# Which queue brings the identity, which transfers lead, and a hold on the first weight casts, in a two-layer attention and pooling block

## The chip, the cores and the metric

One core of a Trainium2 chip runs the whole program in one launch. The metric is device time in microseconds (us) of that launch; the time given for a kernel is the median of its runs. A profile is one further execution, recorded by the hardware profiler.

## What is computed

The reference puts 16 meta tokens ahead of 512 tokens of width 1024 and runs two layers over the 528 rows. Cut to what matters:

```python
h = concatenate([meta, x])                        # 528 x 1024
for l in range(2):
    n    = rms_norm(h, norm_gain[l])              # row / sqrt(mean(row^2) + 1e-6) * gain
    proj = n @ w_in[l]                            # 1024 x 4808, cut into ten parts:
    q, k, v, gate_a, u_b, gate_b, q_idx, k_idx, w_idx, merge = split(proj)
    q, k, q_idx, k_idx = rope(...)                # q and k are normed per head first
    attn = top-128 attention of q over k, v       # keys chosen by the q_idx, k_idx, w_idx scores
    y_a  = (attn * silu(gate_a)) @ w_a[l]
    y_b  = (multiscale_pool(u_b) * silu(gate_b)) @ w_b[l]
    g_a, g_b = split(sigmoid(merge))
    h    = h + (g_a * y_a + g_b * y_b) @ w_out[l]
return h[16:]
```

All in 32-bit floats. [...]

## The kernel before

**Layout.** Activations stand with the features on the partitions and the 528 tokens along the free dimension: `RES[0]` is 128 x 8 x 528, feature block by feature block. Since x comes from memory token by token, it is turned at the start. Tokens are cut into five tiles (`TOK`): tile 0 is the 16 meta tokens, tiles 1 to 4 are 128 tokens of x each, and the work is done in two halves, tiles 0 to 2 and tiles 3 to 4. `xt` holds the four tiles of x as they come from memory, `start` the meta rows and a scratch row for squares, `consts` the tables, whose first 128 columns are the 128 x 128 identity that every turn by TensorE needs.

**First transfers (lines 399 to 434).** SyncE's queue (SP in the profile) issues, in this order: the identity (L405), x tile 1 (L406), x tile 2 (L407), half of the key/value weights `raw` of the chunk `kv` (L156 through `w_fetch(kv, 0)`, two transfers), the rest of the tables (L428), the head gains (L429), the other half of that chunk (two transfers, L156), the two halves of the first index-query chunk `first` (L156, two transfers), and last x tiles 3 and 4 (L434, two transfers). ScalarE's queue (ACTq) issues the meta rows (L408) and the small parameter rows (L409) before ScalarE's first own work, the load of a function table. Each transfer reports on one of eight hardware semaphores, handed out in order of issue over both queues; a transfer that takes a semaphore in use waits on its issuing queue until the earlier transfer on that semaphore has landed.

**Meanwhile** TensorE runs 19 products of zeros (`spin(W0)`, L424) that keep it busy until x is there.

**Start of the work (lines 1163 to 1216).** `x_half(0)` squares and sums the rows of tiles 0, 1 and 2 (ScalarE L1183 and L1179, VectorE for half of tile 2) and takes 1/rms on GpSimd (`inv_rms`, L494 and L495). `x_turned(0)` turns tile 1, then the meta rows, then tile 2 on TensorE, eight transposes each, by way of the identity. `norm_half(0, 0, ...)` spreads 1/rms over the partitions with TensorE and then for each of the eight feature blocks lets VectorE make the normed block `nf` and ScalarE its high part `hhi` (L521); the low parts `hlo` follow on VectorE. The loop at L1209 copies the first 32 tokens of each group of four blocks to `nm` on ScalarE (L1211).

**First weights.** `plain_trio` (L1232) multiplies tiles 0 to 2 by the key/value chunk in plain 32-bit form. `w_prep_enqueue(True)` (L1234) puts the preparation of the chunk `first` in a queue of small steps that `chunk()` empties at L1235: `highs()` (L232) casts both halves to their high parts on ScalarE (`act.copy`, L206), then VectorE subtracts to get the low parts. `w_prep_enqueue` takes an argument `after`: an instruction behind which the scheduler must put these casts (`tc.issue_after`, L233). For this chunk it is not given; for the third chunk it is, at L1253. After that `x_half(1)` and `x_turned(1)` (L1238) do tiles 3 and 4, and the index queries of tiles 1, 2 and so on begin, each `tok_group` of 24 products.

**What sets the order.** TensorE and VectorE run their instructions in the order in which the code writes them (`manual_schedule`, L101). ScalarE, GpSimd and SyncE are ordered by the scheduler of the tile layer, from data dependences, its own estimate of when operands are there, and the edges that `issue_after` adds.

Of the kernel before, what the change touches and what calls it, by code (L numbers as in the profile page):

```python
# [18 lines left out]
NM = 16  # L19
# [72 lines left out]
def tile_block(ctx: ExitStack, tc: tile.TileContext, x, meta, w_in, pool_w, w_a, w_b, w_out, rows, hgain, c_tab, out):  # L92
    nc = tc.nc
    act, gp = nc.scalar, nc.gpsimd
# [8 lines left out]
    def f(ap):  # L103
        return ap.bitcast(F32)
# [53 lines left out]
    def w_load():  # L158
        if W["load"] < len(chunks):
            c = w_place()  # L160
            for s in range(2):
                w_fetch(c, s)
# [10 lines left out]
    def w_tile():  # L173
        return wpool.tile([128, 1024], F32R, tag="w", name="w", bufs=8)

    def w_prep_enqueue(casts_first=False, after=None):
        c = W["prep"]
        if c >= len(chunks):
            return
        W["prep"] += 1  # L180
        kt = chunks[c][0][0].shape[1]
        cols = 2048 // kt
        if c in plain:
            return
        ready[c] = {}
        if c in mixed:
            prep_q.extend(mixed_prep(c))
            return
        parts = ready[c] = ([], [])

        def split(which):
            if c == kept_chunk:
                if which not in own:
                    own[which] = one.tile([128, KT, 256], F32R, tag=("Ahi", "Alo")[which], name="wo")
                i = len(parts[which])
                t = own[which][:, i:i + kt // 2, :]
            else:
                t = w_tile().rearrange("p (k e) -> p k e", e=cols)
            parts[which].extend(t[:, k] for k in range(kt // 2))
            return t  # L200

        his, own = {}, {}

        def high(s):
            his[s] = split(0)
            act.copy(his[s], raws[c][s])  # L206

        def low(s):
            dve.tensor_sub(split(1), raws[c][s], f(his[s]))
            if s == 1:  # L210
                del raws[c]
                w_load()

        def second():
            low(0)
            high(1)

        def minus(s):
            t = split(1)
            act.activation(t, raws[c][s], AF.Copy, scale=-1.0)  # L220
            gp.dma_start(t, raws[c][s], accum_op=OP.add)  # L221

        def plus(s):
            t = split(0)
            act.copy(t, raws[c][s])  # L225
            if s == 1:
                del raws[c]
                w_load()
                with tc.issue_after(added[0]):
                    first_sum(c + 1)  # L230

        def highs():  # L232
            with tc.issue_after(after) if after else nullcontext():  # L233
                high(0)
                high(1)

        if casts_first:
            prep_q.extend((highs, lambda: low(0), lambda: low(1)))
        elif c in by_dma:
            prep_q.extend((lambda: minus(0), lambda: minus(1), lambda: plus(0)))  # L240
            if c in metas:
                prep_q.append(lambda: meta_queries(metas[c], raws[c]))
            prep_q.append(lambda: plus(1))
        else:
            prep_q.extend((lambda: high(0), second, lambda: low(1)))
# [7 lines left out]
    def first_sum(c):  # L253
        if c in mixed:
            gp.dma_start(raws[c][0][:, 1], raws[c][0][:, 0], accum_op=OP.add)  # L255
# [74 lines left out]
    def chunk(ahead=True):  # L330
        flush_prep()
        c = W["use"]
        W["use"] += 1
        if ahead:
            w_prep_enqueue()
        return ready.pop(c)
# [62 lines left out]
    consts = one.tile([128, NCOL], F32, name="consts")  # L399
# [2 lines left out]
    junk, mt = start[:, 0, :], start[:16, 1, :]  # L402
    dma = nc.sync.dma_start
    xt = one.tile([128, 4, D], F32, tag="C", name="xt")
    dma(consts[:, :128], c_tab[:, :128])  # L405
    dma(xt[:, 0, :], x[0, 0:128, :])  # L406
    dma(xt[:, 1, :], x[0, 128:256, :])  # L407
    act.dma_start(mt, meta)  # L408
    act.dma_start(par, rows)  # L409
    warm = one.tile([128, 1], F32, name="warm")  # L410
# [89 lines left out]
    NF = [None]  # L500
    NM = []
# [43 lines left out]
    def meta_queries(g, raw):  # L545
        ps = bank("d")
        by_columns(ps, 256, [(lambda k: NM[k // 4][:, k % 4, :], lambda k: raw[k // 4][:, k % 4, :])])
        dst = qm[:, 4 * g:4 * g + 4, :]
        later(lambda: meta_sum(ps, 256, lambda total: q_post(0, total, True, dst, g)), 1)
# [658 lines left out]

    for b in range(2):  # L1209
        NM.append(tmp.tile([128, 4, 32], F32, tag="pm", name="nm"))  # L1210
        act.copy(NM[b], NF[0][b][:, :, 0:32])  # L1211
    dve.tensor_scalar(psc, parT[:, 24:32], 0.5, None, op0=OP.mult)
    dve.tensor_reduce(fold, ident.rearrange("p (j c) -> p c j", j=4), axis=AX.X, op=OP.add)
    tables(0, True)
# [3 lines left out]
    for l in range(2):  # L1218
# [12 lines left out]
        kv = W["use"] + 1  # L1231
        pss = plain_trio(raws[kv], hooks[0])  # L1232
        if l == 0:
            w_prep_enqueue(True)  # L1234
        w = chunk()  # L1235
        W["use"] += 1
        if l == 0:
# [337 lines left out]
```

## Time and profile before

| | us |
|---|---|
| median of 3 runs | 744.51 |
| lowest and highest run | 743.21, 744.68 |
| the profiled execution, whole | 744.49 |
| its span, first to last instruction | 742.7 |
| TensorE (PE) busy in the span | 732.6 |
| VectorE (DVE) busy | 590.9 |
| ScalarE (ACT) busy | 482.4 |
| GpSimd (POOL) busy | 242.8 |

A row of the timeline reads: start, duration, engine, line, operation, out<-in, how many, and in brackets the idle time of the engine before the row and what ended it. PEld is TensorE's weight load. A name with q behind it (SPq, ACTq) is the engine's sequencer, here issuing a transfer; the duration is that of the issue, not of the transfer. Most operations of TensorE and VectorE go through one helper and so carry its line, L63; their tiles tell them apart. A row of the stretches gives the bounds, the length, each engine's busy time and count, the granted TensorE clock, the mean busy share of the 16 DMA engines, and GB/s. Shares that the packets' times overlap in can pass 1.

### The profile page before, as it was taken

To read this page: it belongs to the slowest core of one execution; us is meant where nothing else is said; L and a number is where in the kernel's file an instruction comes from. 1 tells how busy PE (TensorE), PEld (TensorE's weight loads), DVE (VectorE), ACT (ScalarE), POOL (GpSimd) and SP (SyncE) were. 2 spreads that over 40 slices of the span, in tenths; PEclk is the share of its full clock that TensorE was granted. 3 is DMA by queue.
4 is the path that set the end of the run, shared out by engine and by line. 5 is a ranking of instruction groups with operands and counts; after the bars stand their busy time and mean duration, and the time that the engine had idled before them with its cause. 6 is when DMAs were issued, how large, how long until landed. Compare 5 with 4: busy or idle time off the path is not lost.

```text
span 742.7 us, 16105 instructions
## 1 busy us (share of the span) xinstructions
PE 732.6 (99%) x5949; PEld 705.6 (95%) x5949; DVE 590.9 (80%) x1500; ACT 482.4 (65%) x1099; POOL 242.8 (33%) x320
## 2 busy tenths in 40 slices
PE   8999999999999999999999999999999999999998
PEld 7999999899999999999999989998899999999997
DVE  6876899999897875894449668999989978768874
ACT  6669735656778886543236696367478977865643
POOL 3652173721221310063347410756021222105300
PEclk9999999999999999999999999999999999999999
DMA  8766774864564533543422677659464653448832
GB/s 265 231 154 165 166 158 114 214 158 100 119 139 114 123 64 101 173 156 117 143 88 86 170 171 198 157 128 204 109 156 100 147 111 86 116 107 261 201 89 72
DMA packets 103567, 106.42 MB, mean 143 GB/s; under 512 B 5008, under 2 KB 83632, under 8 KB 103488
## 3 DMA queue, kind: packets, MB, share of 16 engines
q1 hardware_dynamic: 91888, 74.89, 33.4%
q0 software_dynamic: 11520, 30.41, 22.8%
q8 instruction: 47, 0.77, 0.4%
q14 instruction: 32, 0.26, 0.1%
q10 hardware_dynamic: 80, 0.08, 0.0%
HBM read 66.41 MB, written 8.55 MB: 101 GB/s over the span
## 4 chain that ended last, share of the span: by engine, by line
PE 65%; DVE 23%; ACT 5%; issue 2%; DMA 2%; POOL 2%; SPq 1%; DVEq 0%; POOLq 0%; ACTq 0%
PE d L63 52%; PE a L63 9%; DVE sc L63 6%; DVE m L63 4%; PE v L63 4%; DVE w L63 2%; DVE t L63 2%; DMA xt<-in_x_dram 2%; ACT lt L791 1%; DVE lt L63 1%; DVE silb L63 1%; DVE us L63 1%; DVE mlo L63 1%; ACT w L225 1%; DVE qs L63 1%
## 5 line engine op out<-in xcount | busy, mean ns | idle before, releaser
L63 PE MATMUL d<-hhi,w 128*128 128x256 f32 (+3 forms) x1392 | 278.6, 291 | 0.8 <-DVE c L63 0.7
L63 PEld LDWEIGHTS d<-hhi,w 128*128 128x128 f32 x1392 | 222.4, 188 | 3.9 <-DVE c L63 1.2
L63 PE MATMUL d<-hlo,w 128*128 128x256 f32 (+3 forms) x696 | 189.9, 289 | 0.0
L63 DVE TENSOR_TENSOR w<-raw,w 128x512 fp32r<-128x512 f32 (+1 forms) x156 | 121.7, 786 | 20.7 <-ACT w L269 20.3
L63 PEld LDWEIGHTS d<-hlo,w 128*128 128x128 f32 x696 | 131.3, 189 | 1.4 <-issue 0.2
L63 PE MATMUL d<-hsum,w 128*128 128x264 f32 (+1 forms) x720 | 95.9, 285 | 0.6 <-ACT u L1019 0.3
L63 PEld LDWEIGHTS d<-hsum,w 128*128 128x128 f32 x720 | 89.6, 188 | 1.7 <-ACT u L1019 0.8
L63 PE MATMUL d<-w,hhi 128*128 128x256 f32 x576 | 86.1, 287 | 0.7 <-ACT sq L668 0.7
L269 ACT CAST w<-raw 128x512 fp32r<-128x512 f32 x132 | 78.7, 621 | 3.3 <-DMA raw<-s 1.4
L63 PEld LDWEIGHTS d<-w,hhi 128*128 128x128 f32 x576 | 74.7, 188 | 5.2 <-issue 2.3
L255 POOL DMA_DIRECT2D raw<-raw x22 | 19.8, 902 | 114.6 <-DMA raw<-in_w_in_dram 42.8
L221 POOL DMA_DIRECT2D w<-raw x34 | 31.5, 943 | 73.8 <-ACT w L220 51.1
L63 DVE MATCH_REPLACE8 sc<-m,sc 128x400 f32<-128x400 f32 (+2 forms) x100 | 54.5, 549 | 0.0
L791 ACT ACTIVATE lt<-lt,mn,NR 128x144 f32<-128x144 f32 (+3 forms) x64 | 42.2, 661 | 18.2 <-DVE mn L63 18.0
L63 DVE MAX8 m<-sc 128x8 f32<-128x400 f32 (+2 forms) x100 | 53.2, 557 | 0.9
L284 POOL DMA_DIRECT2D raw<-s x22 | 19.3, 879 | 91.0 <-DVE s L63 32.7
L63 DVE SCALAR_TENSOR_TENSOR sc<-r,wsg,sc 128x144 f32<-128x144 f32 (+3 forms) x56 | 32.4, 582 | 17.3 <-ACT r L714 15.0
L63 PE MATMUL d<-w,hlo 128*128 128x256 f32 x288 | 45.5, 281 | 0.0
L63 PE MATMUL d<-mhi,w 128*128 128x272 f32 (+2 forms) x192 | 45.2, 324 | 0.0
L677 POOL TENSOR_TENSOR t<-t,t 128x256 f32<-128x256 f32 (+1 forms) x34 | 32.5, 955 | 26.4 <-DVE t L63 25.0
L1420 POOL TENSOR_TENSOR hlo<-ta,hhi 128x256 fp32r<-128x256 f32 (+1 forms) x28 | 26.8, 966 | 43.6 <-PE d L63 31.4
L806 POOL TENSOR_SCALAR pm<-lt,rs 128x16 f32<-128x16 f32 x48 | 24.6, 573 | 47.3 <-DVE rs L63 47.3
(245 smaller groups left out, 1560.0 us busy)
## 6 DMA issues: line engine op xcount, KB each, us to landing
raw<-in_w_in_dram SPq DMA_DIRECT2D x88, 256.0 KB, 3.5
w<-raw POOLq DMA_DIRECT2D x34, 512.0 KB, 5.9
raw<-in_w_in_dram SPq DMA_DIRECT2D x32, 512.0 KB, 4.4
raw<-in_w_out_dram SPq DMA_DIRECT2D x12, 512.0 KB, 3.8
raw<-raw POOLq DMA_DIRECT2D x22, 256.0 KB, 4.2
raw<-s POOLq DMA_DIRECT2D x22, 256.0 KB, 3.3
kept<-res SPq DMA_DIRECT2D x16, 264.0 KB, 4.1
res<-kept SPq DMA_DIRECT2D x16, 264.0 KB, 6.4
```

The source lines that it names most:

```text
L63: return fn(*a, **k)
L221: gp.dma_start(t, raws[c][s], accum_op=OP.add)
L225: act.copy(t, raws[c][s])
L255: gp.dma_start(raws[c][0][:, 1], raws[c][0][:, 0], accum_op=OP.add)
L269: act.copy(t[:, 0], blk[src[n]])
L284: gp.dma_start(blk["a12"], blk["s2"], accum_op=OP.add)
L677: added[0] = gp.tensor_tensor(t1[:m, :256], t1[:m, :256], t2[:m, :256], op=OP.add).ins
L791: act.activation(L[hh][:, :n], L[hh][:, :n], AF.Exp, scale=NR[:, i, h:h + 1], bias=mn[:, hh:hh + 1], accum_out=sm[:, hh:hh + 1])
L806: (gp if j < 3 else dve).tensor_scalar(pms[i][:, 2 * j + hh, :], L[hh][:, 0:16], rs[:, hh:hh + 1], None, op0=OP.mult)
L1420: pool_end = gp.tensor_sub(hlo[:, j, a:a + n], d, f(hhi[:, j, a:a + n]))
```

## The change

The identity leaves SyncE's queue and goes to the head of ScalarE's, so that the two x tiles are SyncE's first transfers. The last of the two `nm` copies is kept as `begun` and handed to `w_prep_enqueue` for the chunk `first`, so that its two casts stand behind that copy, which itself follows the eight high parts of the normed x.

```diff
     dma = nc.sync.dma_start
     xt = one.tile([128, 4, D], F32, tag="C", name="xt")
-    dma(consts[:, :128], c_tab[:, :128])
     dma(xt[:, 0, :], x[0, 0:128, :])
     dma(xt[:, 1, :], x[0, 128:256, :])
+    act.dma_start(consts[:, :128], c_tab[:, :128])
     act.dma_start(mt, meta)
     act.dma_start(par, rows)
...
     for b in range(2):
         NM.append(tmp.tile([128, 4, 32], F32, tag="pm", name="nm"))
-        act.copy(NM[b], NF[0][b][:, :, 0:32])
+        begun = act.copy(NM[b], NF[0][b][:, :, 0:32]).ins
...
         if l == 0:
-            w_prep_enqueue(True)
+            w_prep_enqueue(True, begun)
```

## The prediction, made before the result was known

> **What bounds the kernel now.** I read the page's busy times first, then the chain that ended last, then the timeline and the DMA of the first 20 us, where all edited lines lie.
>
> ```profile
> PE 732.6 (99%) x5949; PEld 705.6 (95%) x5949; DVE 590.9 (80%) x1500; ACT 482.4 (65%) x1099; POOL 242.8 (33%) x320
> ```
>
> TensorE is busy for 732.6 of 742.7 us. Only about 10 us of the span is time in which it does nothing, so a change at the start can gain only what it takes out of those 10 us. The waits of TensorE after 20 us, longest first (total, times, longest), begin so:
>
> ```profile
> PE d L63 <- DVE c L63: 0.7, 1, 0.7
> PE d L63 <- ACT sq L668: 0.7, 1, 0.7
> ```
>
> No transfer stands in that list. After 20 us TensorE goes from product to product, and what it wins or loses earlier is handed on to the end. So the question is when TensorE gets past its last early wait. The chain of the first 25 us, in order of time (start, us, what):
>
> ```profile
> 0.73 0.39 SPq L405
> 1.11 0.06 issue
> 1.17 4.52 DMA xt<-in_x_dram
> ...
> 8.58 2.61 SPq L434
> 11.19 0.04 issue
> 11.23 8.32 DMA xt<-in_x_dram
> 19.55 0.04 issue
> 19.59 1.09 PE a L63 x8
> ```
>
> Two transfers carry it: x tile 1, issued at 1.17 behind the identity and landed at 1.17 + 4.52 = 5.69, and x tile 4, issued at 11.23 and landed only at 19.55. The second matters more, as the timeline shows:
>
> ```profile
> 0.72 0.42 ACTq L408 DMA_DIRECT2D start<-in_meta_tokens_dram  x1
> 1.17 0.42 SPq L406 DMA_DIRECT2D xt<-in_x_dram  x1
> 1.17 0.44 ACTq L409 DMA_DIRECT2D par<-in_rows_dram  x1
> 1.54 4.42 PE L63 MATMUL d<-idle 128*128 128x256 f32 x19 [1.54 <-DVE ss L63]
> 1.64 1.28 ACT L413 ACT_TABLE_LOAD   x1 [1.64 <-PEq L1561]
> 3.50 1.05 ACT L1183 ACTIVATE start<-start 16x1024 f32<-16x1024 f32 x1
> 4.46 0.19 ACT L1183 ACTIVATION_READ_ACCUMULATOR start<-start 16x1 f32 x1
> 4.92 3.61 SPq L156 DMA_DIRECT2D raw<-in_w_in_dram  x4
> 5.78 1.06 ACT L1183 ACTIVATE start<-xt 128x1024 f32<-128x1024 f32 x1 [1.13 <-DMA xt<-in_x_dram]
> 5.83 1.21 PE L63 MATMUL a<-consts,xt 128*128 128x128 f32 x8
> 13.77 0.29 ACT L1211 COPY nm<-nf 128x128 f32<-128x128 f32 x1
> 14.46 1.04 ACT L206 CAST w<-raw 128x1024 fp32r<-128x1024 f32 x1 [0.41 <-DMA raw<-in_w_in_dram]
> 15.96 1.05 ACT L206 CAST w<-raw 128x1024 fp32r<-128x1024 f32 x1 [0.45 <-DMA raw<-in_w_in_dram]
> 17.33 1.06 PE L63 MATMUL a<-consts,xt 128*128 128x128 f32 x8 [0.23 <-ACT sq L609]
> 19.59 1.09 PE L63 MATMUL a<-consts,xt 128*128 128x128 f32 x8 [1.21 <-DMA xt<-in_x_dram]
> ```
>
> The 19 products of zeros begin at 1.54 and end at 1.54 + 4.42 = 5.96; the turning of x tile 1 begins at 5.83. So TensorE is occupied until the tile is there, and a tile that comes sooner finds it still in the zeros: at most some 0.1 us can be won at this place. Its real wait is the last row: tile 3 is turned by 17.33 + 1.06 = 18.39, and then TensorE stands 1.21 us until tile 4 lands. Whatever shortens the path to 18.39 only lengthens that wait. **The landing of tile 4 is what the change must move.**
>
> What sets that landing is seen in stretches (bounds, length, busy times, clock, DMA share, GB/s):
>
> ```profile
> 1.75:2.50 0.75, 0.75 (x4) 0.75 (x5) 0.00 (x0) 0.75 (x1) 0.00 (x0) 1.00 1.35 255
> 2.50:3.00 0.50, 0.50 (x5) 0.50 (x4) 0.00 (x0) 0.49 (x2) 0.00 (x0) 1.00 0.26 42
> 5.70:7.10 1.40, 1.40 (x12) 1.14 (x11) 0.00 (x0) 1.15 (x2) 0.08 (x1) 1.00 1.09 344
> 7.10:17.50 10.40, 10.05 (x78) 8.72 (x78) 9.73 (x25) 7.69 (x19) 4.48 (x8) 1.00 0.99 319
> 17.50:18.75 1.25, 0.89 (x8) 0.65 (x6) 1.25 (x2) 0.93 (x2) 1.25 (x1) 1.00 0.05 13
> ```
>
> From 5.7 to 17.5 us the DMA engines are full (1.09, then 0.99): one long backlog that drains at 320 to 340 GB/s. Two stretches are not full. At 2.50 to 3.00 the share is 0.26, though both x tiles are issued. And at 17.50 to 18.75 the share is 0.05 of 16 engines, which is less than one engine's work, although tile 4 lands only at 19.55. One engine is late. The DMA view of 17.3 to 18.6 us names its other work (packets, MB, share):
>
> ```profile
> q1 hardware_dynamic: 13, 0.04, 8.5%
> q8 instruction: 1, 0.02, 5.2%
> ```
>
> One packet of queue 8, program code, is moved in that window. At 5.2% of 16 engines over 1.3 us it takes 0.052 x 16 x 1.3 = 1.08 us of one engine, which is the width of the hole. So tile 4 is all but there at 17.5 us, and its last piece waits behind a piece of program.
>
> **The change, part by part.**
>
> *Two x tiles lead.* SyncE loses its first issue, so tile 1's issue moves from 1.17 to 0.73, by 0.44 us, and every later issue of that queue with it. This is the gain, at most 0.44 us, if the DMA stream moves as one. Against it stand the sizes:
>
> ```profile
> consts<-in_tables_dram SPq DMA_DIRECT2D x1, 64.0 KB, 2.5
> start<-in_meta_tokens_dram ACTq DMA_DIRECT2D x1, 64.0 KB, 2.4
> ```
>
> Identity and meta rows are 64 KB each, and before they moved mostly at 1.75 to 2.50, ahead of x. Now they share the engines with x. At the 344 GB/s of the full stretch 64 KB take 65.5/344 = 0.19 us. The net is between 0.44 - 0.38 = 0.06 us (neither hidden) and 0.44 us (both hidden). I hide the identity in the slack stretch, whose share of 0.26 leaves 0.74 x 0.5 = 0.37 us and which I expect behind x's first packets again, and charge the meta rows, issued 0.45 us later than before: 0.44 - 0.19 = **0.25 us**. [...]
>
> *The waits on semaphores.* In the built program each transfer's semaphore moves on by one. The first transfer of the second key/value half waits for x tile 1 to land (before: the identity), and the first half of `first` for x tile 2 (before: the parameter rows). Behind a waiting issue stand all later ones of SyncE, tiles 3 and 4 among them. The row at 4.92 begins with that transfer; now it begins at tile 1's landing, about 5.69 - 0.25 = 5.44, so 0.5 us later than before. What hides this is the backlog: tile 4 issued at 11.23 lands 8.32 us later, so issues run several us ahead of the engines. I cost it at nothing. Without that cover it is the rival that makes the kernel slower, below.
>
> *One issue more on ScalarE.* ScalarE's three issues end about 0.45 us later (0.72 to 1.17 is one), so the table load goes from 1.64 to 2.09, and the meta square, which began at 3.50, to some 3.95; with 1.05 and 0.19 it is done by 5.2. It is queued ahead of tile 1's square, which can begin at 5.44. Slack 0.2 us. If it is gone, 1/rms of the first half is late by that much, and TensorE's later start eats into its 1.21 us at 18.39. Nothing reaches the end.
>
> *The hold.* The built program has the casts exactly where they stood: eight high parts, the second `nm` copy, two casts. The row at 13.77 ends at 14.06, and the first cast waits 0.41 us for its weights until 14.46. With the new order of transfers but without the hold, the scheduler would put the first cast ahead of the last two high parts, where it would wait for those weights. So the hold costs 0, and undoes what the first part would have moved. TensorE, VectorE and GpSimd have the same instructions in the same order.
>
> *The sum.* Tile 4 lands at 19.55 - 0.25 = 19.30. TensorE continues 0.25 us sooner and hands that on: 744.49 - 0.25 = 744.24, or 744.2. The median shown (744.51) is 0.02 above the profiled execution, so no correction is made.
>
> **The rivals.**
>
> *A. The piece of program no longer hits tile 4.* Then tile 4 is there when TensorE is done with tile 3, the 1.21 us are gone, and with the shift the sum is 744.49 - 1.21 - 0.25 = 743.0. For it: the three runs of before spread over 1.47 us, and the lowest, 743.21, is about one such wait below the others. Against it: I take the code to be fetched as TensorE's sequence proceeds; the fetch falls where tile 3's turning begins (17.33), which itself needs tile 3 landed. Tile 3 and tile 4 move together, so the fetch should move with them and hit the same piece. [...]
>
> *B. Identity and meta rows eat the gain*, or the stream's slow start is not tied to the issue: 0.06 us or nothing, 744.4 to 744.5.
>
> *C. SyncE's new waits starve the engines (slower).* Place: the second key/value half, issued 0.5 us later than before, and `first`, which now cannot be issued before tile 2's landing (ScalarE takes that tile at about 7.1, against an issue of `first` at some 6.1). Each delays all issues behind it, so tile 4 comes up to 7.1 - 6.1 = 1.0 us later, and with the code fetch behind it the sum is 744.49 + 1.0 = 745.5. It decides from the moment when the backlog is shorter than the delay. For it: the waits are in the program. Against it: 0.99 share from 7.1 to 17.5 and 8.32 us from issue to landing.
>
> **How the numbers follow.** Forecast (744.2) 0.48, A (743.0) 0.27, B (744.45) 0.15, C (745.5) 0.10. The range goes from A with the whole 0.44 us (744.49 - 1.21 - 0.44 = 742.84) to B (744.5), each end moved out by 0.3 to 0.6 us, since a median of runs that spread over 1.47 us is itself loose by about that: 742.5 to 745.1. Most of C is left out. About 0.2% of 744.5, 1.5 us, is what a measurement of this kernel can tell from no change: the limits are 743.0 and 746.0. A lies on the lower limit, so half of it and a little of the forecast's tail count as faster: 0.18. Slower by that much needs C with a second loss: 0.06. The rest, 0.76, is within.
>
> **What would show it.** In the profile after: SyncE's first row is x tile 1 at about 0.73; tile 1 lands at 5.2 to 5.6, while TensorE still turns it from about 5.8; the casts stand behind the `nm` copy; the DMA share from 5.7 to 17 is near 1 (else C); tile 4 lands near 19.3 and TensorE waits about 1 us for it, with a queue-8 packet in the second before. If that wait is gone, A is right and the forecast's choice was wrong. If tile 4 lands at 19.5 or later with a full DMA, B; with gaps in the DMA share, C. A difference that arises after 25 us would make the whole argument wrong.

## The result, and the profile after

| | before | after |
|---|---|---|
| median, us (14 runs each) | 743.35 | 746.13 |
| lowest and highest run | 743.02, 744.89 | 743.68, 747.13 |
| the profiled execution, whole / span | 744.49 / 742.7 | 746.29 / 743.9 |

The ratio after to before is 1.0025, interval 1.0014 to 1.0037: slower by about 0.25%, 1.9 us. The forecast of 744.2 and its whole range, up to 745.1, lie below. (The medians stand further apart, 1.0037, because after's runs fall in two groups; the means stand 1.0025 apart.) The same kernel was timed again in a later comparison (e5 below), at 1.0012 (1.0003 to 1.0020), 0.9 us; its median there, 744.61, lies inside the range, but again above that of before. So the change costs about 1 to 2 us, and the size itself varies from one comparison to the next; the experiments show that the runs fall in two groups whose mix differs.

The timeline of after, first 22 us (start, us, engine, line, operation, in brackets the idle time before and what ended it):

```profile
0.72 0.41 ACTq L407 DMA_DIRECT2D consts<-in_tables_dram  x1
0.73 0.40 SPq L405 DMA_DIRECT2D xt<-in_x_dram  x1
1.53 3.83 PE L63 MATMUL d<-idle 128*128 128x256 f32 x19 [1.53 <-DVE ss L63]
6.10 0.30 ACT L442 CAST identr<-consts 128x128 fp32r<-128x128 f32 x1 [2.48 <-DMA consts<-in_tables_dram]
6.12 1.09 PE L63 MATMUL a<-consts,xt 128*128 128x128 f32 x8 [0.76 <-DMA consts<-in_tables_dram]
6.78 1.06 ACT L1183 ACTIVATE start<-start 16x1024 f32<-16x1024 f32 x1 [0.38 <-DMA start<-in_meta_tokens_dram]
7.96 1.06 ACT L1183 ACTIVATE start<-xt 128x1024 f32<-128x1024 f32 x1
10.31 0.48 PE L63 MATMUL a<-consts,rstd 16*128 16x16 f32 x2 [1.29 <-POOL rstd L495]
11.37 0.47 PE L63 MATMUL a<-consts,rstd 128*128 128x128 f32 x1 [0.23 <-POOL rstd L495]
11.96 3.36 DVE L63 SCALAR_TENSOR_TENSOR nf<-res,parT,a 128x272 f32<-128x272 f32 x8 [1.85 <-PE a L63]
12.71 6.57 PE L63 MATMUL d<-raw,nf 128*128 128x200 f32 x32
15.67 0.29 ACT L1211 COPY nm<-nf 128x128 f32<-128x128 f32 x1
15.87 1.99 ACT L206 CAST w<-raw 128x1024 fp32r<-128x1024 f32 x2
20.03 1.97 PE L63 MATMUL a<-consts,xt 128*128 128x128 f32 x16
21.75 1.18 PE L63 MATMUL d<-w,hhi 128*128 128x256 f32 x8
```

The rows of before that answer to these and were not shown yet:

```profile
3.30 0.30 ACT L442 CAST identr<-consts 128x128 fp32r<-128x128 f32 x1 [0.16 <-DMA consts<-in_tables_dram]
10.05 3.36 DVE L63 SCALAR_TENSOR_TENSOR nf<-res,parT,a 128x272 f32<-128x272 f32 x8 [0.44 <-PE a L63]
10.60 5.68 PE L63 MATMUL d<-raw,nf 128*128 128x200 f32 x32
20.44 1.20 PE L63 MATMUL d<-w,hhi 128*128 128x256 f32 x8
```

Read from the top. The identity is issued at 0.72, first of all, and its cast on ScalarE can start only at 6.10; before, issued just as early, it was there for a cast at 3.30. TensorE ends the zeros at 1.53 + 3.83 = 5.36 and waits 0.76 us, for the identity and not for x. ScalarE works in order: cast of the identity, then 0.38 us of waiting for the meta rows, which come behind the identity on the same queue, their square, and the square of tile 1, at 7.96 where it was at 5.78. So 1/rms is late, TensorE waits 1.29 and 0.23 us for it, and the normed blocks start at 11.96 instead of 10.05: 1.91 us. Then a second loss that no wait shows: the same 32 key/value products take 6.57 instead of 5.68 us. They end at 19.28 where they ended at 16.28, 3.0 us later. Here the waits of before pay back: tiles 3 and 4 are turned in one go (x16 at 20.03), without the 1.21 us for tile 4 and the 0.23 us for ScalarE's `sq`; a further 0.25 us is overlap between rows that before kept apart. What is left when the first index-query product starts is 21.75 - 20.44 = 1.31 us, and the spans differ by 743.9 - 742.7 = 1.2. Nothing more arises later.

The transfers from ScalarE's queue (KB, us from issue to landing):

```profile
consts<-in_tables_dram ACTq DMA_DIRECT2D x1, 64.0 KB, 5.4
start<-in_meta_tokens_dram ACTq DMA_DIRECT2D x1, 64.0 KB, 5.5
```

Before they took 2.5 and 2.4. The stretches (length, busy times with counts, clock, DMA share, GB/s):

```profile
7.10:17.50 10.40, 8.88 (x53) 8.30 (x52) 7.83 (x21) 8.67 (x20) 3.92 (x7) 0.84 1.04 337
17.50:18.75 1.25, 1.25 (x9) 1.25 (x8) 1.25 (x5) 0.36 (x1) 0.00 (x0) 1.00 0.00 0
7.90:11.30 3.40, 1.95 (x14) 1.44 (x13) 2.10 (x6) 2.86 (x7) 1.83 (x5) 1.00 1.03 317
11.30:14.70 3.40, 3.33 (x12) 3.34 (x13) 2.75 (x7) 2.21 (x7) 2.09 (x4) 0.50 1.11 345
```

The DMA engines stay full until 17.5 (1.04, before 0.99). The last two rows go with the slow products: for 3.4 us the granted clock is 0.50, after 3.4 us in which TensorE was busy for only 1.95.

### The profile page after: what moved, and what is told of

Its sections match the earlier page's. It is cut to its first block, busy times and chain, and to the rows that moved or that the text cites. A ratio compares the mean times of both kernels' runs of the same rounds, so it can differ in the third digit from the quotient of the medians.

```text
span 743.9 us, 16105 instructions
## 1 busy us (share of the span) xinstructions
PE 733.1 (99%) x5949; PEld 706.5 (95%) x5949; DVE 591.1 (79%) x1500; ACT 482.7 (65%) x1099; POOL 242.5 (33%) x320
## 4 chain that ended last, share of the span: by engine, by line
PE 68%; DVE 20%; ACT 5%; issue 3%; DMA 2%; POOL 1%; ACTq 0%; DVEq 0%; SPq 0%; POOLq 0%
PE d L63 55%; PE a L63 10%; DVE sc L63 5%; PE v L63 4%; DVE m L63 3%; DVE w L63 2%; DVE t L63 2%; ACT lt L791 1%; DVE lt L63 1%; DMA raw<-in_w_in_dram 1%; DVE silb L63 1%; DVE us L63 1%; DMA start<-in_meta_tokens_dram 1%; DVE mlo L63 1%; ACT w L269 1%
```

## The experiments

**The theory** after the comparison: the identity is slow because its small pieces take turns with x's large ones; the late identity, and the meta rows behind it, hold up ScalarE's in-order work and with it 1/rms; the idle TensorE is then given half the clock. **The rivals:** the hold on the casts costs; SyncE's new semaphore waits cost (rival C of the prediction); the slow clock is the chip's doing and not the kernel's. The runs stand in three comparisons of four, four and three kernels, each with its own runs of before; e1 to e4 are compared with a median of 743.71, e5 to e8 with 743.68, e9 to e11 with 743.23. The diffs are against after. One view is used throughout: the start of the first index-query row (`d<-w,hhi`), because the span follows it.

### e1, e5, e6: without the hold, and the change once more

e1 and e6 are the same kernel, after without the hold; e5 is after itself. (A high part is the cast of an operand to fp32r, its low part what a subtraction of that leaves; `tok_group` adds up the products high by high, low by high and high by low.)

```diff
-        begun = act.copy(NM[b], NF[0][b][:, :, 0:32]).ins
+        act.copy(NM[b], NF[0][b][:, :, 0:32])
...
-            w_prep_enqueue(True, begun)
+            w_prep_enqueue(True)
```

> The new transfers without the hold (the first cast then stands ahead of the last two high parts). Theory 1, turns: the identity's eight small pieces per DMA engine take turns with x's 4 KB pieces, land at about 6.1 us, and hold up ScalarE's squares by 2 us; the hold has nothing to do with it, so the time is that of the changed kernel, 745 to 746.5. Theory 2, the hold: the loss comes from the casts, and the time goes back to about 743.4.

> The changed kernel once more, beside the same without the hold on one chip. Theory 1: 744.2 when TensorE's clock stays up, 746 to 747 when it falls, and as many of each as the identity's landing decides; if the run without the hold was better only because the identity landed at 4.96 there instead of 6.1, this kernel does as well on the same chip, within 0.5 us of it. If the hold itself costs, this is slower by 1 us or more.

> As before: the new transfers without the hold, now beside the changed kernel on one chip. Theory 1: within 0.5 us of the changed kernel. Theory 2, the hold: faster by 1 us or more.

Medians: e1 743.98, ratio 1.0009 (1.0001 to 1.0018); e5 744.61, 1.0012 (1.0003 to 1.0020); e6 744.89, 1.0012 (1.0002 to 1.0023). With the hold (e5) and without it (e6) in one comparison the medians are equal within 0.3 us, so the hold is not the loss; a share of some tenths of a microsecond these intervals cannot exclude. The profile of e5:

```profile
5.06 0.30 ACT L442 CAST identr<-consts 128x128 fp32r<-128x128 f32 x1 [1.45 <-DMA consts<-in_tables_dram]
7.01 1.06 ACT L1183 ACTIVATE start<-xt 128x1024 f32<-128x1024 f32 x1
10.86 3.35 DVE L63 SCALAR_TENSOR_TENSOR nf<-res,parT,a 128x272 f32<-128x272 f32 x8 [0.82 <-PE a L63]
11.40 5.68 PE L63 MATMUL d<-raw,nf 128*128 128x200 f32 x32
19.55 1.20 PE L63 MATMUL d<-w,hhi 128*128 128x256 f32 x8
```

The identity is late here too, but by 1.8 us and not 2.8, and the clock stayed at 1.00. This execution is even ahead of the profiled one of before (19.55 against 20.44, span 741.8 against 742.7), since that one has the tile-4 wait. So one kernel has several outcomes, and the median is their mix. By the mean granted clock of each run: in 8 of 14 runs of after and 4 of 11 of e5 it is 0.997 or 0.998, with spans from 743.5 to 745.1; in the others it is above, with spans from 741.8 to 742.6. Without the hold it is so in 2 of 11 runs of e1 and 6 of 12 of e6. Of the 91 runs of before in the three comparisons, 4 have the lower clock.

### e9, e7: the same bytes of x in smaller pieces

Tile 1 of x is brought in two transfers with rows of 2 KB (e9), or four with rows of 1 KB (e7). Same bytes, same queues, same order; only the number of SyncE's transfers, and with it who shares a semaphore, changes besides. The edit of e9 (e7 has 256 for each 512):

```diff
-    dma(xt[:, 0, :], x[0, 0:128, :])
+    for c in range(0, D, 512):
+        dma(xt[:, 0, c:c + 512], x[0, 0:128, c:c + 512])
```

> The changed kernel with x tile 1 brought in four transfers of 1 KB rows instead of one of 4 KB rows. Theory 1, turns: the identity's eight pieces per engine now wait for eight 1 KB pieces instead of eight 4 KB pieces, so it lands 0.8 to 1.5 us sooner than in the changed kernel, at 3.5 to 4.8. If the engines share by bytes, or ScalarE's queue is slow by itself, it lands where it did, 5 to 6. The time may be worse all the same, since SyncE issues three transfers more and tile 2 and the weights come later.

> The changed kernel with x tile 1 in two transfers of 2 KB rows. Theory 1, turns: the identity lands between the four-way cut (3.44) and the whole rows (5.03 on that chip), at 3.8 to 4.6. If the number of SyncE's transfers matters and not the size of their rows, it lands where whole rows have it.

Of e9, then of e7, the cast of the identity and the square of tile 1:

```profile
4.25 0.30 ACT L443 CAST identr<-consts 128x128 fp32r<-128x128 f32 x1 [0.64 <-DMA consts<-in_tables_dram]
6.07 1.06 ACT L1184 ACTIVATE start<-xt 128x1024 f32<-128x1024 f32 x1
```

```profile
3.52 0.28 ACT L443 CAST identr<-consts 128x128 fp32r<-128x128 f32 x1
5.22 1.06 ACT L1184 ACTIVATE start<-xt 128x1024 f32<-128x1024 f32 x1
```

With rows of 4, 2 and 1 KB on the other queue, the same 64 KB land at 5.03 (e5), 4.23 and 3.44. Bytes do not explain that: they are the same. Turns do. The packets of SyncE's queue (q1) and ScalarE's (q10) in after from 1.5 to 4.3 us (packets, MB, share):

```profile
q1 hardware_dynamic: 143, 0.55, 54.9%
q10 hardware_dynamic: 111, 0.05, 13.9%
```

and in e9 from 1.5 to 3.4 us:

```profile
q1 hardware_dynamic: 172, 0.33, 55.6%
q10 hardware_dynamic: 143, 0.09, 18.4%
```

The two queues advance by nearly equal numbers of packets (143 to 111, 172 to 143), and by very unequal bytes. Taken in steps of 0.4 us, after has 22 to 12 from 2.6 us, where the identity sets in, 25 to 27 from 3.0, 28 to 26 from 3.4 and 42 to 42 from 3.8; e7 has 95 to 110 from 2.2 us, before ScalarE's queue runs dry. The identity is 128 rows of 512 B; each of them stands behind about one row of x, which in after is eight times its size. In after the median record from 1.5 to 6.2 us is 27 ns for a piece of 512 B and 159 ns for one of 4 KB.

Times: e9 743.19, ratio 0.9993 (0.9984 to 1.0003); e7 743.19, 0.9999 (0.9990 to 1.0007). No run of either has the lower clock, and the loss is gone. Each leaves the queues, the order and the hold of the change as they are, so none of these is the loss.

### e2, e8: the identity not against x

e2 puts the meta rows at the head of SyncE's queue, ahead of x, and leaves the identity and the small parameters on ScalarE's. e8 puts the identity on SyncE's queue again, behind tile 1, and the cast `identr`, which nothing needs early, behind the `nm` copies.

The edit of e2, then of e8:

```diff
+    dma(mt, meta)
     dma(xt[:, 0, :], x[0, 0:128, :])
...
-    act.dma_start(mt, meta)
```

```diff
     dma(xt[:, 0, :], x[0, 0:128, :])
+    dma(consts[:, :128], c_tab[:, :128])
     dma(xt[:, 1, :], x[0, 128:256, :])
-    act.dma_start(consts[:, :128], c_tab[:, :128])
...
-    act.copy(identr, ident)
...
+    with tc.issue_after(begun):
+        act.copy(identr, ident)
```

> The identity still leads ScalarE's queue, but the meta rows lead SyncE's, so that x is issued 0.44 us later as in the kernel before. Theory 1, turns: the identity is through before x's pieces arrive, lands at 3.1 to 3.6, and the time is that of before, 743.4 within 0.4. Rival, slow queue: a transfer from ScalarE's queue lands late by itself, near 6, and the time stays at 745 or more.

> x tile 1 leads SyncE's queue and the identity follows it there, ahead of tile 2; the meta rows lead ScalarE's queue; the rounded copy of the identity is made later. Theory 1: within one queue the identity comes right behind tile 1, both by 5.5, TensorE starts turning at 5.6 to 5.9 as before, tile 1's square at 5.3 to 5.6, and the time is 742.8 to 743.7, no worse than before. If it is the lead of x that costs, whatever the queue, the time is 744.2 or more.

Of e2, then of e8:

```profile
3.22 0.30 ACT L442 CAST identr<-consts 128x128 fp32r<-128x128 f32 x1
4.98 1.06 ACT L1183 ACTIVATE start<-xt 128x1024 f32<-128x1024 f32 x1 [0.42 <-DMA xt<-in_x_dram]
5.76 1.25 PE L63 MATMUL a<-consts,xt 128*128 128x128 f32 x8
18.74 1.19 PE L63 MATMUL d<-w,hhi 128*128 128x256 f32 x8
```

```profile
5.54 1.06 ACT L1182 ACTIVATE start<-xt 128x1024 f32<-128x1024 f32 x1
5.75 1.05 PE L63 MATMUL a<-consts,xt 128*128 128x128 f32 x8
18.42 1.19 PE L63 MATMUL d<-w,hhi 128*128 128x256 f32 x8
```

In e2 the identity is as early as before and tile 1 is squared 0.8 us earlier than before (4.98 against 5.78). That is no gain of the order, for x is issued at 1.17 in both: in the profile of before 5 of the 16 engines brought their share of the tile 0.4 us or more behind the other 11 (by 5.08, then from 5.49 to 5.69), and in e2 all 16 were done by 4.90. TensorE does not use it either, for behind its zeros it starts to turn the tile at 5.76 (before 5.83). In e8 the identity comes with the tile and nobody waits for it. Times: e2 743.30, 0.9996 (0.9987 to 1.0006); e8 743.22, 0.9995 (0.9986 to 1.0003). Both undo the loss, neither is measurably faster than before, and neither has a run with the lower clock.

### e3, e10: the clock by itself

e3 adds eight products of zeros where TensorE waits for 1/rms; e10 takes away the eight that stand there already. What these products give is used by nothing.

The edits stand in `norm_half`, e3 first:

```diff
         rb = bank("a")
+        if warm_up:
+            spin(8)
```

```diff
-            if warm_up and t == 2:
-                spin(3)
...
-        if warm_up:
-            spin(5)
```

> The changed kernel with eight more products of zeros where TensorE stood for 1.4 us before the first 1/rms. Theory 1 with its second half (the idle stretch makes the clock fall to half for one window in about half of the runs): the granted clock is 1.00 or 0.999 in every run, no run is above 745.5, and the median is 744.2 within 0.5. If the clock is not what lifts runs to 746 and more, the median stays within 0.5 of the changed kernel's.

> The changed kernel without the three and five products of zeros that stand around the first spreads of 1/rms, so that TensorE stands idle longer at 9 to 11.5 us. Clock theory: the dose goes up from the changed kernel's (12 of 25 runs with a mean clock of 0.998 or less; none of 12 with the fill), so more than half of the runs, 7 or more of 11, show it, and these runs are 1.5 to 3 us longer than the rest; median 745 to 746.5. If the clock falls by chance and not through idle time, the share stays at or under a half and the median at 744 to 744.9.

e3, stretches before and after 11.3:

```profile
7.90:11.30 3.40, 3.11 (x22) 2.45 (x20) 1.45 (x5) 2.06 (x6) 2.58 (x6) 1.00 1.08 327
11.30:14.70 3.40, 3.32 (x21) 3.18 (x20) 3.40 (x10) 3.20 (x10) 1.34 (x2) 1.00 1.10 365
```

e10, the same and its products:

```profile
7.73:11.13 3.40, 2.44 (x20) 1.83 (x20) 1.86 (x5) 2.12 (x6) 2.51 (x6) 1.00 1.07 326
11.14:14.56 3.42, 3.15 (x9) 3.15 (x10) 3.42 (x10) 3.17 (x9) 1.38 (x2) 0.50 1.10 361
```

```profile
10.86 3.35 DVE L63 SCALAR_TENSOR_TENSOR nf<-res,parT,a 128x272 f32<-128x272 f32 x8 [0.71 <-PE a L63]
11.41 7.21 PE L63 MATMUL d<-raw,nf 128*128 128x200 f32 x32 [0.67 <-DVE nf L63]
21.09 1.18 PE L63 MATMUL d<-w,hhi 128*128 128x256 f32 x8
```

With filler no run of 12 has the lower clock, without those eight 5 of 5, with the change as it is 12 of 25 (after and e5). So the clock is the kernel's doing: it depends on what TensorE has to do around the wait for 1/rms. Whether it is the idle time or the missing products that counts, these two runs do not separate; the last section comes back to it. And e10 prices it, since it starts its normed blocks at 10.86 exactly as e5 does: 7.21 against 5.68 us for the products, `d<-w,hhi` at 21.09 against 19.55, spans 743.3 against 741.8. The low clock in that place cost 1.5 us there. Medians: e3 744.08, 1.0005 (0.9995 to 1.0014); e10 745.55, 1.0036 (1.0022 to 1.0050). With the identity late but the clock kept, e3 is level with before: most of the measured loss is the clock.

### e4, e11: two misses

e4 keeps the two queues but puts the meta rows ahead of the identity, and the cast `identr` late as in e8, so that ScalarE's squares do not stand behind the identity. e11 is e8 with the rest of the tables moved behind x tiles 3 and 4, to bring those tiles sooner.

The edit of e4 in the order of the transfers, and that of e11 beside e8:

```diff
-    act.dma_start(consts[:, :128], c_tab[:, :128])
     act.dma_start(mt, meta)
+    act.dma_start(consts[:, :128], c_tab[:, :128])
```

```diff
     w_fetch(kv, 0)
-    dma(consts[:, 128:], c_tab[:, 128:])
...
         dma(xt[:, t, :], x[0, t * 128:(t + 1) * 128, :])
+    dma(consts[:, 128:], c_tab[:, 128:])
```

> x still leads SyncE's queue; ScalarE's queue brings the meta rows first and the identity second, and the rounded copy of the identity is made later, so that ScalarE's squares need only the meta rows and x. Theory 1: the meta rows (one piece per DMA engine) land at 3 to 4.5, the identity still at about 6, tile 1's square starts at 5.5 to 6.2 instead of 7.96, TensorE waits only the 0.8 us for the identity, and the time is 743.4 to 744.2. Rival, SyncE's waits: SyncE still waits for the identity before the rest of the first weights, so the time stays at 745 to 746.5.

> The run with x tile 1 and the identity on one queue, with the 420 KB rest of the tables moved behind x tiles 3 and 4. Tile 4 then lands over 1 us sooner, 420 KB at some 340 GB/s, so no piece of program can hold it beyond the end of tile 3's turning. If the two kinds of runs of the kernel before (spans near 741.2 and near 742.6) differ by that wait, the upper kind is gone here and the median is 742.3 to 743.1, better than both kernels. If the later tables hold up the rotary products instead, the time is 743.5 or more.

e4: 744.59, ratio 1.0013 (1.0001 to 1.0025). The squares are back where they were (tile 1 at 5.52), but the identity, second in its queue, is later still, and TensorE waits for it:

```profile
6.94 1.94 PE L63 MATMUL a<-consts,xt 128*128 128x128 f32 x8 [0.99 <-DMA consts<-in_tables_dram]
```

The eight turns take 1.94 us here, 1.05 in e8, although the clock column reads 1.00 in both. In the profiled run the turns of tile 2 take 1.97 as well; the products speed up only at about 14.5 us, where the trace's record of the clock begins. Spans fall into three groups: 741.3 to 741.8 (6 runs), 743.0 and 743.3, and 744.5 to 744.6 (4). A faster ScalarE did not help; the idle time had moved to another place, and there TensorE stayed slow.

e11: 744.27, 1.0017 (1.0008 to 1.0025). Tiles 3 and 4 are turned sooner, and TensorE reaches the index queries first of all kernels. But GpSimd's scaled tables come late, and behind them 1/rms of the second half:

```profile
18.24 1.20 PE L63 MATMUL d<-w,hhi 128*128 128x256 f32 x8
19.07 0.87 POOL L485 TENSOR_TENSOR Cg<-consts,gk 128x320 f32<-128x320 f32 x1
21.95 0.43 PE L63 MATMUL a<-consts,rstd 128*128 128x128 f32 x2 [0.62 <-POOL rstd L494]
```

The wait shown is 0.62 us, the span is 1.5 us longer than e8's. The rest is a second wait of TensorE, 0.98 us for VectorE's `w` at 43.45; e8 has neither. Why VectorE is late there was not followed back.

### What holds the runs together

Start of `d<-w,hhi` and span of the profiled execution:

| kernel | starts, us | span, us | difference |
|---|---|---|---|
| e8 identity behind tile 1 | 18.42 | 740.8 | 722.4 |
| e2 identity against nothing | 18.74 | 741.0 | 722.3 |
| e9 halves / e7 quarters | 18.88 / 19.03 | 741.0 / 741.1 | 722.1 / 722.1 |
| e5 the change, clock kept | 19.55 | 741.8 | 722.3 |
| e3 the change, filled | 19.67 | 742.1 | 722.4 |
| before | 20.44 | 742.7 | 722.3 |
| e10 no zeros, clock lost | 21.09 | 743.3 | 722.2 |
| after, clock lost | 21.75 | 743.9 | 722.2 |
| e4 meta rows first, slow start | 22.38 | 744.6 | 722.2 |
| e11 tables late | 18.24 | 742.3 | 724.1 |

All but e11 run on for 722.1 to 722.4 us from that point (e1 and e6, at 19.52 and 19.71, too). But for e11, the whole case is decided before it.

## Why the prediction was wrong

**The step that failed** is the price of the identity: "At the 344 GB/s of the full stretch 64 KB take 65.5/344 = 0.19 us", and after it "I hide the identity in the slack stretch". It prices a transfer by its bytes and asks only how long x is held up. What counted was how long the identity itself is held up, for it is needed first. In its place the runs showed 2.8 us in after (cast at 6.10 against 3.30) and 1.8 in e5, set by the number of turns and the size of the other queue's rows, 0.2 us when those are 1 KB (e7). The meta rows, charged with the same 0.19 us, took 5.5 us to land instead of 2.4. Nor was there a slack stretch to hide in: from 2.50 to 3.50 us the DMA share of after is 0.89 (before 0.35).

**The gain on the x tiles** came and bought nothing. Tile 1 landed at 5.79 in the profile of after (before 5.69), but at 4.66 in that of e5, 1.0 us sooner, part of it because before had five late engines; tile 4 at 18.07 and 17.30, against 19.55 in before and 19.30 in the forecast. So "The landing of tile 4 is what the change must move" was answered, by more than was forecast, and the time still went up: TensorE and ScalarE waited for the identity and the meta rows, and TensorE reached tile 3 only at 20.03.

**ScalarE** was seen as the risk: "Slack 0.2 us. If it is gone, 1/rms of the first half is late by that much ... Nothing reaches the end." The order was right, the size was 2.2 us (7.96 against 5.78). The step reckoned only with the later issue; the cast of the identity (6.10 to 6.40) and then the meta rows (square at 6.78 instead of some 3.95) held ScalarE up, and it counted neither as a wait. That TensorE's later start would eat into the 1.21 us of tile 4 was right; that nothing reaches the end was not: 1.3 us did.

**The clock** is a term the sum lacked. The prediction read 1.00 in each row and took it as given. The mean granted clock was 0.997 or 0.998 in 8 of 14 runs of after and 4 of 11 of e5, and in the profile of after it was 0.50 from 11.30 to 14.70; in e10 the low clock cost 1.5 us, and in the profile of after the 32 products took 0.9 us longer.

**The base of the sum**, 744.49, was an execution with the tile-4 wait; the median of 14 runs of before is 743.35. Measured from there, the forecast of 744.2 would itself be a loss of 0.9 us, so its nearness to e5's 744.61 is luck.

**Rival A** (tile 4 no longer held up by a piece of program) was right in its mechanism and not in its sum. In before 15 of 16 engines had reported tile 4 by 18.44 and the last did at 19.55, and one packet of queue 8 took 1.08 us from 17.36. The same packet is in the traces of after, e1, e2, e5 and e8 (0.96 to 1.08 us, starting from 16.4 to 17.2). That the code comes as TensorE goes on is in the traces from the second such packet on: it starts after 202 products in before and 203 in after, the third after 346 in both. The first one, which matters here, did not keep to that (17.36 after 104 products, 17.15 after 76), so here it did not move with tile 3. In these five traces the last engine is at most 0.4 us behind the one before it. So in after the wait is gone twice over: the tile is there at 18.07, and TensorE is late. In before itself the runs stand in two groups, spans of 740.6 to 741.7 and, apart from the four at the lower clock, of 741.9 to 742.9. The distance is the size of this wait, but the one execution of before with a profile is of the upper group, so that the wait makes the groups is inferred. It also means that a change can lose 1.2 us ahead of tile 4 and look harmless beside an upper run. **Rival B** (gain eaten) was right that there was no gain and had no loss in it. **Rival C** expected SyncE to wait for x tiles 1 and 2. The new wait that the trace shows is for the late identity, and it had no price:

```profile
SPq L429 <- DMA consts<-in_tables_dram: 2.1, 1, 2.1
```

The trace's rows of the issues name eight semaphores for these transfers, in order of issue over both queues: in after 99 for the identity, 101 and 104 for the two x tiles, and 99 again for the ninth transfer, the head gains, which is issued at 6.10, when the last engine has reported the identity at 6.08. SyncE waits 2.1 us for the semaphore of the late identity, yet the DMA share stays at 1.04 until 17.5 us and tile 4 is there at 18.07, before TensorE wants it. The backlog hid it, as the prediction's working had it.

**The hold** at nothing was right (e5 against e6), although its reason was not quite: without it the first cast goes ahead of the last high parts (it starts at 13.74 in e1, before the second `nm` copy) and does not wait for its weights there. **That all arises before 25 us** was right.

What stays open: why the identity landed at 6.08 in the first profile and near 5.0 in those of e1, e3, e5, e6 and e10, which issue it at the same time. The trace narrows it: in after 8 of the 16 engines reported the identity by 4.64 and the others from 5.24 to 6.08, and tile 1 likewise (by 4.41, then from 5.00 to 5.79); in e5 all 16 reported the identity from 4.42 to 5.03. So half of the engines ran late in that one execution; what held them is not shown. Open too are what the clock counts and why VectorE is late in e11. A version that is measurably faster than before was not found: e2, e7, e8 and e9 are level with it.

## What to carry to other kernels

Here a small transfer on a second queue was priced by the rows that it took turns with, not by its bytes: 64 KB landed at 5.03 us against rows of 4 KB (e5) and at 3.44 against rows of 1 KB (e7). So the first thing that everybody needs is tried ahead of the large rows on one queue (before: cast of the identity at 3.30), or the large rows are cut (e7: at 3.52). Before a transfer is moved to another engine's queue, ask what that engine does next in order, for the wait went to all of it here: ScalarE squared tile 1 at 7.96 in after, at 5.78 in before. And a gap on TensorE cost more than its length where the clock fell after it (0.50 for 3.42 us in e10, where the 32 products took 7.21 us and in e5 5.68); look at the granted clock and at the duration of the same product in both kernels before looking for a wait.

## What the runs showed of the hardware

**The two queues took turns piece by piece.** 64 KB in rows of 512 B landed at 5.03 (e5), 4.23 (e9) and 3.44 us (e7) against rows of 4, 2 and 1 KB, with packet counts of 143 to 111 (after) and 172 to 143 (e9).

**The clock fell after a stretch with few products; what it counts is open.** The clock was 0.50 for 3.40 us in after and for 3.42 in e10. TensorE was busy for 1.95 of 3.40 us ahead of that stretch in after and 2.44 of 3.40 in e10, with no single gap over 1.3 us; at 3.11 (e3) it did not fall. But it did not fall either after 2.13 of 3.40 in e1 and 2.19 in e6, in the same stretch, nor after 1.98 of 3.41 in before (16.37 to 19.78). So busy time alone does not decide. The stretch of e10 held turns and spreads and not one product of zeros or weights, and in e4 a stretch filled with turns (7.65 to 11.06, busy for all of it) left TensorE slow: the five zeros that follow take 1.42 us, in before 0.83. Whether turns count as products do, no run tests.

**The clock column missed the start.** The products of zeros of e4 that start by 5.4 us, and the eight that e3 adds from 8.20 on (count, busy us, mean ns of one):

```profile
L63 PE MATMUL d<-idle 128*128 128x256 f32 x18 | 4.2, 424 | 1.5 <-DVE ss L63 1.5
```

```profile
L63 PE MATMUL d<-idle 128*128 128x256 f32 x8 | 1.2, 293 | 0.0
```

Per product that is 4.2/18 = 0.23 us at the start and 1.2/8 = 0.15 us later, both at a stated 1.00. The traces say why: their records of the clock begin at 4.49 us in after, 6.13 in before, 7.73 in e10 and 14.47 in e4, and ahead of the first record the column shows 1.00. In e10 eight turns take 1.91 us at 5.75 and 1.09 at 8.23, on either side of that point. The duration of one known product was the safer reading here.
